# An RMSNorm-and-swish kernel: larger row groups, a first small store, and a different split of the squares

## The chip, the cores and the metric

The kernel runs on one core of one Trainium2 chip. The metric is the device time of one execution in microseconds (us). Of the kernel before, eight executions were timed: median 160.46 us, from 160.32 to 160.62.

## The reference

The input x has 16 x 1024 rows of 512 float32 values, 16,384 rows or 33.55 MB; the output has the same size. Each row is normalized by its root mean square, scaled by gamma and passed through swish:

```python
rms = np.sqrt(np.mean(x ** 2, axis=-1, keepdims=True) + eps)
x_norm = x / rms * gamma
return (x_norm * (1.0 / (1.0 + np.exp(-x_norm)))).astype(np.float32)
```

Every value is read once and written once, so 67.1 MB cross between HBM and SBUF.

## The kernel before, in words

**Tiles.** The 16,384 rows are 128 partitions times 128 rows. A tile of `sz` rows takes `128 * sz` neighbouring rows of x, of which each partition holds `sz` neighbours: one run of `sz` x 2 KB in HBM and in SBUF. There are eleven tiles, `sizes = [4, 4, 8] + [16] * 6 + [8, 8]` (line 30), each with one load and one store. All live in one ring buffer in SBUF, `xb`, with room for 96 rows per partition. The first eight tiles fill it; the last three (16, 8 and 8 rows) reuse room of earlier tiles, and their loads wait until the stores of those tiles have landed (`load`, lines 108 to 118).

**Chunks.** Computing goes by chunks of `cn = 4` rows per partition, 32 in all. For each chunk k:

- ScalarE squares one row with its accumulator, so that the sum of squares comes with it (line 159, scratch output `junk`), and squares the other `n_sq = 3` rows into PSUM (line 166, `sq`, two buffers).
- VectorE sums these three rows (`sums`, line 204).
- GpSimd adds eps (line 141) and raises to the power -1/2 (line 148).
- VectorE multiplies each of the four rows by its factor and by gamma (`norm`, line 215, four instructions).
- ScalarE applies swish in place (`swish`, line 178).

**Order.** It is written out by hand, one program per engine, with semaphores between them. ScalarE runs `square(k)`, then any store that is due, then `swish(k-2)` (lines 192 to 199). VectorE runs `sums(k)`, then `norm(k-1)` (lines 223 to 233). So the squares of a chunk run ahead of the swish of the chunk two before.

**Queues.** SyncE issues all loads, in the order of the tiles, on queue q1; the first two are placed ahead of the program's opening barrier. ScalarE issues all stores on queue q10, each when the last chunk of its tile has been through swish (`store`, line 181). Ahead of these, ScalarE's queue brings gamma (line 186): four copies of it to four partitions of `gamma4`, which GpSimd has set to zero first (line 136). VectorE spreads them over all partitions with a shuffle (line 228), which stands in its program right after `sums(0)` and before everything else; it waits for gamma's landing (`s_gld`).

At the end SyncE waits for the stores that no load has waited for (lines 236 to 238).

Of the kernel before, what the change touches and what calls it, by code (L numbers as in the profile page):

```python
# [8 lines left out]
@with_exitstack  # L9
def kernel(  # L10
    ctx: ExitStack,
    tc: tile.TileContext,
    x: bass.AP,
    gamma: bass.AP,
    eps: bass.AP,
    out: bass.AP,
):
    nc = tc.nc
    P = nc.NUM_PARTITIONS
    AF = mybir.ActivationFunctionType  # L20
    ALU = mybir.AluOpType
    fp32 = mybir.dt.float32
    bf16 = mybir.dt.bfloat16

    xf = x.flatten_outer_dims()
    of = out.flatten_outer_dims()
    R, D = xf.shape


    sizes = [4, 4, 8] + [16] * 6 + [8, 8]  # L30
    ring = 96
    early = 2
    cn = 4
    n_sq = 3
    N = sum(sizes)
    assert N * P == R, (N, R)


    tiles = []
    done = 0  # L40
    for sz in sizes:
        assert done % ring + sz <= ring
        tiles.append((done * P, sz, done % ring))
        done += sz
    T = len(tiles)

    chunks = [
        (t, r, r == at)
        for t, (_, sz, at) in enumerate(tiles)
        for r in range(at, at + sz, cn)  # L50
    ]
    K = len(chunks)
    ends = []
    e = 0
    for sz in sizes:
        e += sz // cn
        ends.append(e)

    inv_d = 1.0 / float(D)
    eps_f = float(eps)  # L60

    tc.close()
    tc.compile()  # L65

    def sbuf(name, shape, dt=fp32):
        return nc.alloc_sbuf_tensor(name, shape, dt).ap()

    xb = sbuf("xb", [P, ring, D])  # L70
    gamma4 = sbuf("gamma4", [P, D])
    gamma_sb = sbuf("gamma_sb", [P, D])
    junk = [sbuf(f"junk{i}", [P, D], bf16) for i in range(2)]
    neg_half = sbuf("neg_half", [P, cn])
    ms = sbuf("ms", [P, K, cn])
    aeps = sbuf("aeps", [P, K, cn])
    rstd = sbuf("rstd", [P, K, cn])
    sq = [nc.alloc_psum_tensor(f"sq{i}", [P, 4, D], fp32).ap() for i in range(2)]

    ld = [nc.alloc_semaphore(f"ld{t}") for t in range(T)]  # L80
    st = [nc.alloc_semaphore(f"st{t}") for t in range(T)]
    s_gld = nc.alloc_semaphore("s_gld")
    s_zero = nc.alloc_semaphore("s_zero")
    s_half = nc.alloc_semaphore("s_half")
    s_gamma = nc.alloc_semaphore("s_gamma")
    s_acc = nc.alloc_semaphore("s_acc")
    s_sq = nc.alloc_semaphore("s_sq")
    s_sum = nc.alloc_semaphore("s_sum")
    s_eps = nc.alloc_semaphore("s_eps")
    s_rstd = nc.alloc_semaphore("s_rstd")  # L90
    s_norm = nc.alloc_semaphore("s_norm")
    s_swish = nc.alloc_semaphore("s_swish")

    def need(ins, sem, value):
        return ins.wait_op(sem, value, "sem-ge")

    def dram(ap, t):
        first, sz, _ = tiles[t]
        return ap[first : first + P * sz].rearrange("(p n) d -> p n d", n=sz)

    def buf(t):
        _, sz, at = tiles[t]
        return xb[:, at : at + sz, :]


    stored_by_sync = set()

    def load(t):
        _, sz, at = tiles[t]
        waits = [  # L110
            u for u in range(t)
            if tiles[u][2] < at + sz and at < tiles[u][2] + tiles[u][1]
            and u not in stored_by_sync
        ]
        for u in waits:
            nc.sync.wait_ge(st[u], 16)
            stored_by_sync.add(u)
        return nc.sync.dma_start(out=buf(t), in_=dram(xf, t)).then_inc(ld[t], 16)  # L118

    entry = nc.main_func.blocks[0].instructions  # L120
    here = nc.cur_bb.bb.instructions
    for t in range(early):
        ins = load(t).ins
        assert here[-1] is ins or here[-1].name == ins.name
        here.pop()
        at = next(
            i for i, other in enumerate(entry)
            if other.engine == mybir.EngineType.SP
            and isinstance(other, mybir.InstDrain)
        )  # L130
        entry.insert(at, ins)
    for t in range(early, T):
        load(t)


    nc.gpsimd.memset(gamma4, 0.0).then_inc(s_zero, 1)  # L136
    nc.gpsimd.memset(neg_half, -0.5).then_inc(s_half, 1)  # L137
    nc.gpsimd.wait_ge(s_half, 1)
    for k in range(K):
        need(  # L140
            nc.gpsimd.tensor_scalar(  # L141
                out=aeps[:, k, :], in0=ms[:, k, :], scalar1=eps_f, scalar2=None,
                op0=ALU.add,
            ),
            s_sum, k + 1,
        ).then_inc(s_eps, 1)
        need(
            nc.gpsimd.tensor_tensor(  # L148
                out=rstd[:, k, :], in0=aeps[:, k, :], in1=neg_half, op=ALU.pow
            ),  # L150
            s_eps, k + 1,
        ).then_inc(s_rstd, 1)


    def square(k):
        t, at, first = chunks[k]
        if first:
            nc.scalar.wait_ge(ld[t], 16)  # L158
        acc = nc.scalar.activation(  # L159
            out=junk[k % 2], in_=xb[:, at + n_sq, :], func=AF.Square,  # L160
            scale=inv_d**0.5, accum_out=ms[:, k, n_sq : n_sq + 1],
        )
        if k >= 2:
            need(acc, s_acc, k - 1)
        acc.then_inc(s_acc, 1)
        square = nc.scalar.activation(  # L166
            out=sq[k % 2][:, 0:n_sq, :], in_=xb[:, at : at + n_sq, :],
            func=AF.Square, scale=inv_d**0.5,
        )
        if k >= 2:  # L170
            need(square, s_sum, k - 1)
        square.then_inc(s_sq, 1)

    def swish(k):
        _, at, _ = chunks[k]
        rows = xb[:, at : at + cn, :]
        need(
            nc.scalar.activation(out=rows, in_=rows, func=AF.Silu), s_norm, k + 1  # L178
        ).then_inc(s_swish, 1)

    def store(t):
        need(
            nc.scalar.dma_start(out=dram(of, t), in_=buf(t)), s_swish, ends[t]
        ).then_inc(st[t], 16)

    need(
        nc.scalar.dma_start(out=gamma4[0:P:32, :], in_=gamma.partition_broadcast(4)),
        s_zero, 1,
    ).then_inc(s_gld, 16)
    nc.scalar.preload_act_table_set("silu_and_others")  # L190
    stored = 0
    for k in range(K + 3):
        if k < K:
            square(k)
        while stored < T and ends[stored] <= k - 2:
            store(stored)
            stored += 1
        if 2 <= k < K + 2:
            swish(k - 2)


    def sums(k):
        need(
            nc.vector.tensor_reduce(  # L204
                out=ms[:, k, 0:n_sq], in_=sq[k % 2][:, 0:n_sq, :], op=ALU.add,
                axis=mybir.AxisListType.X,
            ),
            s_sq, k + 1,
        ).then_inc(s_sum, 1)

    def norm(k):
        _, at, _ = chunks[k]
        for j in range(cn):
            row = xb[:, at + j, :]
            ins = nc.vector.scalar_tensor_tensor(  # L215
                out=row, in0=row, scalar=rstd[:, k, j : j + 1], in1=gamma_sb,
                op0=ALU.mult, op1=ALU.mult,
            )
            if j == 0:
                need(ins, s_rstd, k + 1)  # L220
        ins.then_inc(s_norm, 1)

    for k in range(K + 1):
        if k < K:
            sums(k)
        if k == 0:
            need(
                nc.vector.stream_shuffle(gamma_sb, gamma4, [0] * 32), s_gld, 16  # L228
            ).then_inc(s_gamma, 1)
        if k == 1:  # L230
            nc.vector.wait_ge(s_gamma, 1)
        if k >= 1:
            norm(k - 1)


    for t in range(T):
        if t not in stored_by_sync:
            nc.sync.wait_ge(st[t], 16)

# [34 lines left out]
```

## Time and profile before

The profiled execution took 160.32 us; its span, from the first to the last instruction, is 159.0 us, so 1.32 us lie around it.

| What | Value |
|---|---|
| Median of 8 executions | 160.46 us |
| Profiled execution, its span | 160.32 us, 159.0 us |
| VectorE: norm, line 215, 128 times | 87.1 us, 737 ns each |
| VectorE: sum of three rows, line 204, 32 times | 55.8 us, 1744 ns each |
| ScalarE: swish of four rows, line 178, 32 times | 61.1 us, 1908 ns each |
| ScalarE: squares of three rows, line 166, 32 times | 45.9 us, 1433 ns each |
| ScalarE: square of one row and its accumulator's read, line 159, 32 times | 19.7 + 6.0 us, 615 + 186 ns each |
| DMA, mean over the span | 422 GB/s |
| ScalarE waiting for VectorE's norm | 17.6 us in 30 waits |
| VectorE waiting for ScalarE's squares | 9.8 us in 3 waits |
| SyncE waiting for stores ahead of the ring's reuse | 55.8 us (first), 18.9 us (second) |

How to read it: "busy" is the time in which an engine executes; DMA rows give the share in which the 16 DMA engines move packets, and the rate. A packet is one row run of one partition. The chain that ended last is followed back from the last instruction to whatever released each step. PE is not used.

### The profile page before, as it was taken

The page shows a single profiled execution, that of the slowest core. Times are in us where ns is not written, and L with a number is a line of the kernel's source. Part 1 is how long each engine was busy: PE and PEld are TensorE (multiplying, and loading weights), DVE is VectorE, ACT ScalarE, POOL GpSimd, SP SyncE. Part 2 cuts the span into 40 slices and gives each one's busy share as a digit, 9 for nine tenths or more (in the row PEclk, how much of TensorE's full clock was granted, in tenths as well). Part 3 has the DMA queues.
Part 4 walks back from the last instruction along what each step waited for, and adds up shares of the span by engine and source line. Part 5 has one row for each costly group of instructions (what it writes and reads, how often), then busy time and mean ns, then how long its engine had stood idle before and what let it go on. Part 6 is the DMA issues. An engine that isn't in the chain of part 4 may idle for free.

```text
span 159.0 us, 437 instructions
## 1 busy us (share of the span) xinstructions
DVE 139.2 (88%) x162; ACT 125.1 (79%) x129; POOL 78.6 (49%) x70
## 2 busy tenths in 40 slices
DVE  0298986999999999999999999999999999998600
ACT  1839839888888998888888888899888888883420
POOL 1043551445555554444444555555488888998100
DMA  6999989999989999999999999999999999999997
GB/s 260 435 495 396 396 371 480 402 422 453 437 367 482 449 416 431 437 437 404 445 429 439 437 445 412 412 457 433 433 416 429 433 441 453 420 429 437 400 412 309
DMA packets 3179, 67.14 MB, mean 422 GB/s; under 512 B 356, under 2 KB 356, under 8 KB 360
## 3 DMA queue, kind: packets, MB, share of 16 engines
q1 hardware_dynamic: 1584, 33.56, 49.8%
q10 hardware_dynamic: 1592, 33.56, 49.1%
q14 instruction: 3, 0.02, 0.0%
HBM read 33.56 MB, written 33.55 MB: 422 GB/s over the span
## 4 chain that ended last, share of the span: by engine, by line
DVE 76%; DMA 13%; ACT 2%; POOL 2%; issue 0%; SPq 0%; ACTq 0%
DVE xb L215 47%; DVE ms L204 29%; DMA xb<-in_x_dram 13%; POOL aeps L141 2%; ACT xb L178 1%; ACT sq L166 1%; POOL rstd L148 1%; ACT junk L159 0%; SPq L118 0%; ACTq L158 0%
## 5 line engine op out<-in xcount | busy, mean ns | idle before, releaser
L215 DVE SCALAR_TENSOR_TENSOR xb<-xb,rstd,gamma_sb 128x512 f32<-128x512 f32 x128 | 87.1, 737 | 1.2 <-POOL rstd L148 1.2
L178 ACT ACTIVATE xb<-xb 128x2048 f32<-128x2048 f32 x32 | 61.1, 1908 | 17.6 <-DVE xb L215 17.6
L141 POOL TENSOR_SCALAR aeps<-ms 128x4 f32<-128x4 f32 x32 | 36.6, 1144 | 64.6 <-DVE ms L204 64.6
L204 DVE TENSOR_REDUCE ms<-sq 128x3 f32<-128x1536 f32 x32 | 55.8, 1744 | 9.9 <-ACT sq L166 9.8
L166 ACT ACTIVATE sq<-xb 128x1536 f32<-128x1536 f32 x32 | 45.9, 1433 | 0.0
L148 POOL TENSOR_TENSOR rstd<-aeps,neg_half 128x4 f32<-128x4 f32 x32 | 41.2, 1288 | 2.7
L159 ACT ACTIVATE junk<-xb 128x512 bf16<-128x512 f32 x32 | 19.7, 615 | 5.9 <-DMA xb<-in_x_dram 5.9
L159 ACT ACTIVATION_READ_ACCUMULATOR junk<-xb 128x1 f32 x32 | 6.0, 186 | 0.0
L190 ACT ACT_TABLE_LOAD x1 | 1.3, 1283 | 3.6 <-issue 3.6
L136 POOL MEMSET gamma<- 128x512 f32 x1 | 0.5, 524 | 1.5 <-POOLq L65 1.5
L228 DVE STREAM_SHUFFLE gamma_sb<-gamma 128x512 f32<-128x512 f32 x1 | 0.7, 721 | 0.0
L255 POOL MEMSET const-float32-0.0<- 128x1 f32 x1 | 0.1, 98 | 0.2 <-issue 0.2
L255 POOL MEMSET const-uint8-127<- 128x1 uint8 x1 | 0.1, 103 | 0.0
L255 POOL MEMSET const-bfloat16-1.0<- 128x1 bf16 x1 | 0.1, 101 | 0.0
L137 POOL MEMSET neg_half<- 128x4 f32 x1 | 0.1, 101 | 0.0
L255 POOL MEMSET const-float32-1.0<- 128x1 f32 x1 | 0.1, 98 | 0.0
L228 DVE LOAD_MASK_SELECT gamma_sb<-gamma x1 | 0.0, 14 | 0.0
## 6 DMA issues: line engine op xcount, KB each, us to landing
xb<-in_x_dram SPq DMA_DIRECT2D x6, 4096.0 KB, 44.0
out_dram<-xb ACTq DMA_DIRECT2D x6, 4096.0 KB, 29.6
xb<-in_x_dram SPq DMA_DIRECT2D x3, 2048.0 KB, 37.7
out_dram<-xb ACTq DMA_DIRECT2D x3, 2048.0 KB, 10.1
xb<-in_x_dram SPq DMA_DIRECT2D x2, 1024.0 KB, 5.8
out_dram<-xb ACTq DMA_DIRECT2D x2, 1024.0 KB, 19.9
gamma<-in_gamma_dram ACTq DMA_DIRECT2D x1, 8.0 KB
```

The costliest lines, as they stand in the source:

```text
L136: nc.gpsimd.memset(gamma4, 0.0).then_inc(s_zero, 1)
L137: nc.gpsimd.memset(neg_half, -0.5).then_inc(s_half, 1)
L141: nc.gpsimd.tensor_scalar(out=aeps[:, k, :], in0=ms[:, k, :], scalar1=eps_f, scalar2=None, op0=ALU.add,),
L148: nc.gpsimd.tensor_tensor(out=rstd[:, k, :], in0=aeps[:, k, :], in1=neg_half, op=ALU.pow),
L159: acc = nc.scalar.activation(out=junk[k % 2], in_=xb[:, at + n_sq, :], func=AF.Square, scale=inv_d**0.5, accum_out=ms[:, k, n_sq : n_sq + 1],)
L166: square = nc.scalar.activation(out=sq[k % 2][:, 0:n_sq, :], in_=xb[:, at : at + n_sq, :], func=AF.Square, scale=inv_d**0.5,)
L178: nc.scalar.activation(out=rows, in_=rows, func=AF.Silu), s_norm, k + 1
L190: nc.scalar.preload_act_table_set("silu_and_others")
L204: nc.vector.tensor_reduce(out=ms[:, k, 0:n_sq], in_=sq[k % 2][:, 0:n_sq, :], op=ALU.add, axis=mybir.AxisListType.X,),
L215: ins = nc.vector.scalar_tensor_tensor(out=row, in0=row, scalar=rstd[:, k, j : j + 1], in1=gamma_sb, op0=ALU.mult, op1=ALU.mult,)
L228: nc.vector.stream_shuffle(gamma_sb, gamma4, [0] * 32), s_gld, 16
L255: nc = _bacc.Bacc("TRN2", target_bir_lowering=False, num_devices=1)
```

## The change

- **A scratch transfer.** An SBUF tile `blank` of 128 x 16 float32 is set to zero by GpSimd, as its first instruction. ScalarE's queue writes it to a scratch tensor in HBM ahead of gamma's transfer: 8 KB, 64 bytes per partition. SyncE waits for its landing after it has issued all loads.
- **Groups, loads and stores.** Rows are laid out in five groups of 16, 48, 32, 16 and 16 rows per partition. A load or a store moves a piece of a group: nine loads of 4, 4, 8, 16, 16, 16, 32, 16 and 16 rows; eight stores of 16, 32, 16, 16, 16, 16, 8 and 8 rows. The 32-row ones have runs of 64 KB per partition. A load waits for those stores that hold the room it will fill.
- **Squares.** In each third chunk (k % 3 == 2, ten of 32) ScalarE squares two rows with the accumulator, and two into PSUM for VectorE to sum; in the others one and three as before. The accumulator's semaphore is split in two, one per `junk` buffer.

```diff
-    sizes = [4, 4, 8] + [16] * 6 + [8, 8]
+    groups = [16, 48, 32, 16, 16]
     ring = 96
+    loads = [(0, 0, 4), (0, 4, 4), (0, 8, 8), (1, 0, 16), (1, 16, 16), (1, 32, 16),
+        (2, 0, 32), (3, 0, 16), (4, 0, 16)]
+    stores = [(0, 0, 16), (1, 0, 32), (1, 32, 16), (2, 0, 16), (2, 16, 16), (3, 0, 16),
+        (4, 0, 8), (4, 8, 8)]
     early = 2
     cn = 4
-    n_sq = 3
...
+    def n_sq(k):
+        return 2 if k % 3 == 2 else 3
...
+    scratch = nc.dram_tensor("scratch", [P, 16], fp32, kind="Internal").ap()
+    blank = sbuf("blank", [P, 16])
...
+    nc.sync.wait_ge(s_scratch, 16)
...
+    nc.gpsimd.memset(blank, 0.0).then_inc(s_blank, 1)
     nc.gpsimd.memset(gamma4, 0.0).then_inc(s_zero, 1)
...
     def square(k):
-        t, at, first = chunks[k]
-        if first:
-            nc.scalar.wait_ge(ld[t], 16)
-        acc = nc.scalar.activation(
-            out=junk[k % 2], in_=xb[:, at + n_sq, :], func=AF.Square,
-            scale=inv_d**0.5, accum_out=ms[:, k, n_sq : n_sq + 1],
-        )
-        if k >= 2:
-            need(acc, s_acc, k - 1)
-        acc.then_inc(s_acc, 1)
+        at, landing = chunks[k]
+        for i in landing:
+            nc.scalar.wait_ge(ld[i], 16)
+        n = n_sq(k)
+        for j in range(n, cn):
+            acc = nc.scalar.activation(
+                out=junk[j % 2], in_=xb[:, at + j, :], func=AF.Square,
+                scale=inv_d**0.5, accum_out=ms[:, k, j : j + 1],
+            )
+            last = acc_on[j % 2]
+            if last:
+                need(acc, s_acc[j % 2], last)
+            acc.then_inc(s_acc[j % 2], 1)
+            acc_on[j % 2] += 1
         square = nc.scalar.activation(
-            out=sq[k % 2][:, 0:n_sq, :], in_=xb[:, at : at + n_sq, :],
+            out=sq[k % 2][:, 0:n, :], in_=xb[:, at : at + n, :],
             func=AF.Square, scale=inv_d**0.5,
         )
...
+    need(nc.scalar.dma_start(out=scratch, in_=blank), s_blank, 1).then_inc(
+        s_scratch, 16
+    )
     need(
         nc.scalar.dma_start(out=gamma4[0:P:32, :], in_=gamma.partition_broadcast(4)),
         s_zero, 1,
```

## The prediction

> **What bounds the kernel now.** I read the engine shares first, then the DMA rows, then the chain that ended last, then windows and the timeline. From the page:
>
> ```profile
> DVE 139.2 (88%) x162; ACT 125.1 (79%) x129; POOL 78.6 (49%) x70
> ...
> DMA  6999989999989999999999999999999999999997
> ...
> q1 hardware_dynamic: 1584, 33.56, 49.8%
> q10 hardware_dynamic: 1592, 33.56, 49.1%
> ...
> DVE 76%; DMA 13%; ACT 2%; POOL 2%; issue 0%; SPq 0%; ACTq 0%
> ```
>
> The chain names VectorE, but the 16 DMA engines are busy 49.8 + 49.1 = 98.9% of the span: two limits stand nearly level. The windows (length, busy us of DVE, ACT and POOL, clock, DMA share, GB/s) say which of them sets the end:
>
> ```profile
> 17.00:21.00 4.00, 4.00 (x5) 3.04 (x2) 1.81 (x2) 1.00 1.01 362
> ...
> 30.00:100.00 70.00, 70.00 (x81) 62.75 (x65) 32.73 (x32) 1.00 1.01 434
> ...
> 152.00:154.00 2.00, 0.00 (x0) 0.24 (x1) 0.00 (x0) 1.00 0.94 401
> ```
>
> In 30 to 100 us both are full, at 434 GB/s. The last store leaves ScalarE's queue at 152.3 us, when the store before it still has packets until 153.8; DMA work never runs out but for a dent at 152 to 154. So the bytes set the end: 67.14 MB at 433 GB/s is 155.1 us. The trace's packet records have the first packet at 1.0 us and the last semaphore at 158.6, 0.4 before the span ends. The 3.5 us that are not bytes at full rate are: 1.0 before the first packet; about 0.8 of slow first packets up to 5 us; (433-362)/433 x 4 = 0.66 at 17 to 21; (433-401)/433 x 2 = 0.15 at 152 to 154; and 0.9 of smaller dents, packet overhead and the stagger of the engines' last packets (158.0 to 158.6).
>
> The dent at 17 to 21 follows the first store, issued at 16.21 to 16.57. The records show load packets of 32 KB, elsewhere 1213 ns, stretched up to 1985 ns on all 16 engines from 17.3 us, and the first store packet at 20.2. Gamma's small transfer, first on the same queue, left no such dent.
>
> [...] between 24 and 44 us, with loads of 32 KB rows and stores of 8 KB rows, the queues' shares are
>
> ```profile
> q1 hardware_dynamic: 231, 7.05, 82.0%
> q10 hardware_dynamic: 226, 1.65, 19.6%
> ```
>
> as many packets of each, so 4 to 1 in bytes.[...] gamma (issue over at 3.54, packet at 7.05) and the first store show about 3.6 under load, and I use 3.5.
>
> **The change part by part.**
>
> *Row sizes.* The packets took 309, 611 and 1213 ns for 8, 16 and 32 KB: 9 ns of overhead each and 36.7 ns per KB of 1000 B. Per engine, before has 32 packets of 8 KB and 48 of 16 KB; after, 16 and 24. Against 32 KB rows an 8 KB packet costs 23/4 ns too much and a 16 KB packet 4.5, so 0.09 + 0.11 us are saved. The 16 packets of 64 KB, extrapolated to 2417 ns, save 9 ns each, 0.14. No trace has a 64 KB row: at worst it runs at the rate of 32 KB rows (0), at best as said. I take -0.34.
>
> *Scratch transfer.* It adds 128 packets of 64 B, 8 per engine. The nearest row is the 4 B semaphore packet at 9 ns[...]. Estimate 8 x 11 = 0.09 us.[...] The wait on it by SyncE stands after all loads are issued (near 98 us), when it has long landed: 0.
>
> *The dent.* If the 0.66 us belong to the first write to HBM, the scratch transfer takes them with 64 B in flight instead of 8 KB rows, and they shrink to nothing or fall into the first 5 us. If they belong to a queue that starts anew beside loads, they stay, or come twice, since after the change the store queue runs empty once more. Bounds: -0.66 to +2.3 (rival C). I take -0.66, because the stretched packets end where the first write lands, and the last store, which finds that queue empty on some engines, shows no stretched packets (it has no loads beside it, which weakens this).
>
> *Two rows for three on VectorE.* Ten of 32 chunks (k = 2, 5, ... 29) reduce two rows instead of three. The reduction takes 1744 ns for 1536 elements, so about 533 less for 1024. ScalarE adds 0.61 (a square with accumulator and its read: 130.90 to 131.51 in the timeline) and saves 1908 - 1433 = 475 ns, the rows' price of 512 elements: +0.14. Now the loop from the end of a norm over swish and squares to the next reduction:
>
> ```profile
> 129.08 1.91 ACT L178 ACTIVATE xb<-xb 128x2048 f32<-128x2048 f32 x1 [0.46 <-DVE xb L215]
> 130.90 0.61 ACT L159 ACTIVATE junk<-xb 128x512 bf16<-128x512 f32 x1
> 131.42 0.19 ACT L159 ACTIVATION_READ_ACCUMULATOR junk<-xb 128x1 f32 x1
> 131.51 1.43 ACT L166 ACTIVATE sq<-xb 128x1536 f32<-128x1536 f32 x1
> 133.40 1.91 ACT L178 ACTIVATE xb<-xb 128x2048 f32<-128x2048 f32 x1 [0.45 <-DVE xb L215]
> ```
>
> ScalarE needs 3.98 of VectorE's 4.315 us (1.67 + 2.65 in the chain). With a short reduction VectorE needs 3.78 and ScalarE's 3.98 decides: 0.33 gained per such chunk, 9 of them between sums(4) and sums(31), 3.0 us. A chunk with two accumulated rows needs 4.12, still under 4.315. GpSimd's two steps end 1.30 after the norm before (the scale's addition overhangs by 0.15, then 0.09 and 1.04), later than a short reduction's 1.14, but 1.30 + 2.65 stays within the 3.98. The two accumulator semaphores add no work. This gain lies behind the full DMA; it only brings the last store forward, closing the dent at 152: -0.15.
>
> *Gamma, moved behind the scratch transfer.* ScalarE's queue issues the scratch transfer at about 2.05 (after a 0.1 us memset) to 3.1, if the first issue takes gamma's 1.09; then gamma's, and ScalarE starts some 0.4 later than 4.87. First scratch packet at 3.1 + 3.5 = 6.6. Its 8 packets and its semaphore each wait out one load packet: 8 turns of 0.61 + 0.01 to 11.6, then gamma and its semaphore at 1.21 each: 14.0, seen at 14.3, instead of 7.8. Queued behind the shuffle on VectorE is everything: shuffle 0.72, sums 1.68, norm 2.65, sums 1.14, norm 2.65, sums 1.67, norm 2.65, so sums(4) at 14.3 + 13.2 = 27.5 instead of 25.4. Then 27 periods, 116.5 - 3.0 = 113.5, and 10.3 from sums(31) to the last store (152.27 - 141.99): issue at 151.3 instead of 152.3. Cover: DMA has other stores queued. With 4.85 for 2.1 MB, 0.85 to the first packet and 0.4 to the end of the span, VectorE's chain alone would end the span at gamma + 143.1 = 157.4.
>
> *Loads and stores.* Store 0 (16 rows) waits for chunk 3, about 34 us, and shares evenly with the loads, then 1 to 2 with the 64 KB load; it lands by 58. The 32-row store waits for chunk 11: sums(12) at 27.5 + 8 x 4.2 = 61.1, norm and swish to 67. Bytes by 68 are (68 - 2) x 0.433 = 28.6 MB; less 4.2 of store 0 that is 24.4 of the 25.2 for the first 96 rows, and the 32-row load lands near 72 at half rate. Chunk 16 squares at 27.5 + 12 x 4.2 - 2.05 = 75.9: some 4 us of cover. The big store (8.4 MB, two thirds of 433 after 72) lands near 99; the last load, which SyncE holds until then, follows at half rate, 19.4 us, near 121; chunk 28 squares near 126. Both covers are thin, and a late load costs only beyond the 0.5 us between 157.4 and the bytes' end, as the queues never stand empty.
>
> Sum: 159.0 - 0.34 + 0.09 - 0.66 - 0.15 = 157.9 of span, 159.3 with the 1.32 around it (profiled 160.32). The median, 160.46, is 0.14 above: 159.4.
>
> **Rivals.**
> B, the dent stays, at store 0 or around the scratch transfer: 0.66 back, 160.1. For it: one dent in either kernel. Against it: the scratch transfer has 64 B per packet.
> C, slower: every start of the store queue beside loads dents, at store 0 (33 us) and at the 32-row store (66 us). Each costs 0.66, up to half of the 3 us before the first write, 1.5, as the queues now share evenly. A's 159.4 has none of them, so this is 159.4 + 1.3 to 3.0, 160.7 to 162.4, likely 161. It turns slower once the dents sum to over 1.4. Gamma's silence speaks against it, but gamma writes no HBM.
> D, slower: gamma lands late and VectorE's chain sets the end, at gamma + 143.1 of span. It decides over the bytes from 14.8 us on, and the kernel is slower from 16.2; at 18, 161.1 + 1.5 = 162.6. For it: nothing lies between VectorE and that wait. Against it: the scratch packets would have to wait two turns each.
> That 5.3 us of reduction saved shorten the kernel by as much, to 157, needs bytes at over 433 GB/s; no chance.
>
> **How the numbers follow.** A 0.46 (159.4; 159.1 to 159.8), B 0.20 (160.1; 159.8 to 160.4), C 0.18, D 0.16. The bound of what the measurement tells is 0.2%, 0.32 us: faster is under 160.14, slower over 160.78. A, a half of B and 0.01 of D are faster, 0.57; the other half of B and 0.06 of C the same, 0.16; the rest slower, 0.27. The range from 159.0 to 161.3 leaves out C's and D's upper parts.
>
> **What would show it.** Right: no dent near 33 us; the GB/s rows at 433 until the last store; VectorE's idle time larger (waiting for gamma by some 5 us, for ScalarE by 0.2 in each third chunk); the reduction of two rows near 1.2 us; ScalarE never waiting for the 32-row load. Wrong: dents after 33 and 66 us (C); the shuffle later than 15 us, or a gap in DMA before the last store (D); a wait for loads of over 2 us at chunk 16 or 28.

## The result and the profile after

The changed kernel takes 162.80 us (median of 11 executions, 161.20 to 163.55) against 160.40 for the kernel before: a ratio of 1.0137, with a 95% interval from 1.0116 to 1.0159. It is slower, where 159.4 us and a gain of 0.7% were forecast, and it lies outside the range of 159.0 to 161.3. Its executions also spread over 2.3 us, those of before over 0.65. Every ratio here is formed from all executions but those more than 1.5% above the fastest of the same kernel, so it need not be the quotient of the two medians beside it; the one of the changed kernel takes in a twelfth execution, of 161.87 us.

The profiled execution took 162.08 us, its span 160.8. From the page of the changed kernel: engine shares, DMA, queues, the chain that ended last.

```profile
DVE 134.5 (84%) x162; ACT 126.4 (79%) x149; POOL 65.4 (41%) x71
...
DMA  7999999999999989989999998999999999999992
...
q1 hardware_dynamic: 1296, 33.56, 49.4%
q10 hardware_dynamic: 1304, 33.57, 48.5%
...
DVE 55%; ACT 25%; DMA 5%; issue 4%; another core or an unknown queue 3%; POOL 0%; ACTq 0%; POOLq 0%
```

VectorE lost 4.7 us of work, and the DMA engines were busy for 97.9% of a longer span. Summed over the 16 engines the packets took 157.29 us per engine, exactly as before (157.29): the mean DMA engine had no more to do. The chain names VectorE and ScalarE, as it follows the last instruction back and does not ask which DMA engine landed last. The last digit of the DMA row, 7 before and 2 after, is the first hint. The windows of the tail show it (length, busy us of DVE, ACT, POOL, clock, DMA share, GB/s), first of the kernel before:

```profile
157.00:158.60 1.60, 0.00 (x0) 0.00 (x0) 0.00 (x0) 1.00 0.48 205
158.60:162.00 3.40, 0.00 (x0) 0.00 (x0) 0.00 (x0) 1.00 0.00 0
```

and then of the changed kernel:

```profile
157.00:158.60 1.60, 0.00 (x0) 0.00 (x0) 0.00 (x0) 1.00 0.29 123
158.60:160.80 2.20, 0.00 (x0) 0.00 (x0) 0.00 (x0) 1.00 0.03 15
```

In the changed kernel most engines are done earlier, and something goes on after 158.6 us at a twentieth of the rate or less. The packet records of the trace say what: the last store's semaphores come from 15 engines between 157.4 and 158.5 us, and from one at 160.39. One engine of 16, a late engine, ends 2.6 us after the median one.

Two more windows of the changed kernel, for the dent after the first real store:

```profile
17.00:21.00 4.00, 3.85 (x5) 4.00 (x5) 2.02 (x2) 1.00 0.91 393
33.00:37.00 4.00, 4.00 (x6) 3.31 (x5) 2.04 (x2) 1.00 1.07 369
```

Windows of 4 us count whole packets, so that their GB/s wander; the packet records are sharper. A packet is called stretched where it takes longer than its usual 309, 611, 1213 or 2418 ns for 8, 16, 32 or 64 KB. The records show no stretched packet at 14 to 24 us in the changed kernel (0.66 us per engine before) and 0.91 us per engine at 30 to 40. The dent has moved to the new first store, issued at 30.4, and has grown.

Last, ScalarE at chunk 16, which needs the 32-row load, and VectorE behind it (timeline; in brackets the idle time ahead and what ended it):

```profile
76.63 0.63 ACT L178 ACTIVATE junk<-xb 128x512 bf16<-128x512 f32 x1 [4.55 <-DMA xb<-in_x_dram]
...
78.72 1.76 DVE L229 TENSOR_REDUCE ms<-sq 128x3 f32<-128x1536 f32 x1 [4.04 <-ACT sq L187]
```

The load lands at 76.2 us. Its last packet had ended at 73.8; the semaphore packet behind it waited out one store packet of 64 KB, 2.4 us. Even so the last store leaves at 150.98, earlier than before (152.27): this stall is not yet what sets the end.

### The profile page after: what moved, and what is told of

It is laid out like the page before. It is cut to its first block, busy times and chain, and to the rows that moved or that the text cites. A ratio compares the mean times of both kernels' runs of the same rounds, so it can differ in the third digit from the quotient of the medians.

```text
span 160.8 us, 451 instructions
## 1 busy us (share of the span) xinstructions
DVE 134.5 (84%) x162; ACT 126.4 (79%) x149; POOL 65.4 (41%) x71
## 4 chain that ended last, share of the span: by engine, by line
DVE 55%; ACT 25%; DMA 5%; issue 4%; another core or an unknown queue 3%; POOL 0%; ACTq 0%; POOLq 0%
DVE xb L240 35%; DVE ms L229 20%; ACT xb L199 12%; ACT sq L187 9%; DMA gamma<-in_gamma_dram 5%; ACT junk L178 4%; DVE gamma_sb L253 0%; POOL gamma L151 0%; POOL blank L150 0%; ACTq L175 0%; POOLq L69 0%
## 5 line engine op out<-in xcount | busy, mean ns | idle before, releaser
L199 ACT ACTIVATE xb<-xb 128x2048 f32<-128x2048 f32 x32 | 60.9, 1904 | 12.9 <-DVE xb L240 12.9
L229 DVE TENSOR_REDUCE ms<-sq 128x3 f32<-128x1536 f32 (+1 forms) x32 | 50.7, 1586 | 12.5 <-ACT sq L187 11.0
L156 POOL TENSOR_SCALAR aeps<-ms 128x4 f32<-128x4 f32 x32 | 20.6, 644 | 76.1 <-DVE ms L229 76.1
L163 POOL TENSOR_TENSOR rstd<-aeps,neg_half 128x4 f32<-128x4 f32 x32 | 44.0, 1376 | 2.7
L187 ACT ACTIVATE sq<-xb 128x1536 f32<-128x1536 f32 (+1 forms) x32 | 41.6, 1299 | 0.0
L178 ACT ACTIVATE junk<-xb 128x512 bf16<-128x512 f32 x42 | 25.8, 615 | 8.0 <-DMA xb<-in_x_dram 8.0
L178 ACT ACTIVATION_READ_ACCUMULATOR junk<-xb 128x1 f32 x42 | 7.8, 187 | 0.0
```

What stands on the lines that cost most here:

```text
L156: nc.gpsimd.tensor_scalar(out=aeps[:, k, :], in0=ms[:, k, :], scalar1=eps_f, scalar2=None, op0=ALU.add,),
L163: nc.gpsimd.tensor_tensor(out=rstd[:, k, :], in0=aeps[:, k, :], in1=neg_half, op=ALU.pow),
L178: acc = nc.scalar.activation(out=junk[j % 2], in_=xb[:, at + j, :], func=AF.Square, scale=inv_d**0.5, accum_out=ms[:, k, j : j + 1],)
L187: square = nc.scalar.activation(out=sq[k % 2][:, 0:n, :], in_=xb[:, at : at + n, :], func=AF.Square, scale=inv_d**0.5,)
L229: nc.vector.tensor_reduce(out=ms[:, k, 0 : n_sq(k)], in_=sq[k % 2][:, 0 : n_sq(k), :], op=ALU.add, axis=mybir.AxisListType.X,),
```

## The experiments

All ratios are against the kernel before, with 95% intervals; the changed kernel stands at 1.0137. Times are medians unless a single execution is named.

### Which part of the change

**Without the scratch transfer.** The four lines that write it, wait for it and clear its source are taken out.

```diff
-    need(nc.scalar.dma_start(out=scratch, in_=blank), s_blank, 1).then_inc(
-        s_scratch, 16
-    )
```

> The changed kernel without the scratch transfer. The changed kernel stands at 1.014 of before; in its profile 15 DMA engines end at 157.4 to 158.1 us and one at 160.4. Theory S (the scratch transfer brings the late engine): 1.003 or less. Theories R (the 64 KB rows bring it) and F (the first real store, now 16 rows of 32 KB, brings it): 1.012 to 1.016, the late engine still 2 us or more behind the rest.

Measured: 163.01 us, 1.0152 (1.0107 to 1.0197). Two engines end late, the last 3.4 us after the median. Theory S falls.

**The squares as before.**

```diff
-        return 2 if k % 3 == 2 else 3
+        return 3
```

> The changed kernel with three rows summed by VectorE in every chunk, as before. S, R and F: the split of the squares is not the cause, 1.012 to 1.018, the upper end because the last store then leaves some 2 us later. If the denser ScalarE program is the cause: 1.004 or less.

Measured: 161.73 us, 1.009 of the 160.23 us of the kernel before beside it; the 20 executions lie anywhere from 160.3 to 164.0, and the 12 below 162.7 alone give 1.0052 (1.0031 to 1.0072). Neither expectation fits: the split of the squares is not needed for the loss, since half of it or more remains in 11 of the 20, but six stay below 161 us, where the changed kernel has none of 12. This version comes back below.

**The 32-row pieces split.**

```diff
-        (2, 0, 32), (3, 0, 16), (4, 0, 16)]
-    stores = [(0, 0, 16), (1, 0, 32), (1, 32, 16), (2, 0, 16), (2, 16, 16), (3, 0, 16),
+        (2, 0, 16), (2, 16, 16), (3, 0, 16), (4, 0, 16)]
+    stores = [(0, 0, 16), (1, 0, 16), (1, 16, 16), (1, 32, 16), (2, 0, 16), (2, 16, 16), (3, 0, 16),
```

> The changed kernel with the 32-row load and the 32-row store each split in two of 16 rows; the layout of the groups stays. R: 0.998 to 1.004, the late engine gone. S and F: 1.012 to 1.016.

Measured: 160.60 us, 1.0018 (1.0009 to 1.0027), 160.2 to 161.2. Most of the loss is gone with the 64 KB rows, and so is the tail:

```profile
157.00:158.60 1.60, 0.00 (x0) 0.00 (x0) 0.00 (x0) 1.00 0.58 246
158.60:162.00 3.40, 0.00 (x0) 0.00 (x0) 0.00 (x0) 1.00 0.00 0
```

**The scratch transfer alone, added to the kernel before.**

> The kernel before with the scratch transfer alone added. S: 1.008 or more, with one late engine. R and F: 0.998 to 1.003, gamma's shuffle about 2 us later as in the changed kernel (10.8 us), and the dent at 17 to 21 us still there at about 0.66 us, since the dent after the first store stayed in the changed kernel.

Measured: 160.24 us, 0.9996 (0.9985 to 1.0008): nothing. One of its 12 executions, not in the ratio, took 162.51 us, as long as the changed kernel and without any 64 KB rows; it was not profiled, so its cause is open. The dent did change, against the expectation: at 14 to 24 us it fell from 0.66 to 0.28 us per engine. But the stretched packets of the first 10 us rose from 0.41 to 0.68, and those at 43 to 49 from 0.09 to 0.36. All in all the packets of this profile are stretched by 1.66 us per engine, those of before by 1.41. In these profiles, one of each kernel, the transfer moves the loss about and takes none away.

**The split of the squares alone, added to the kernel before.**

> The kernel before with the changed split of the squares alone (two rows summed by VectorE in each third chunk). If DMA sets the end, as the prediction has it: 0.996 to 1.001, the last store issued 1 to 3 us earlier and the time not following. If VectorE sets it: 0.980 to 0.988.

Measured: 160.39 us, 0.9990 (0.9979 to 1.0002). The last store leaves at

```profile
148.35 0.34 ACTq L192 DMA_DIRECT2D out_dram<-xb  x1
```

3.9 us before the 152.27 of the kernel before, and the time does not follow. So DMA sets the end of the kernel before, as the prediction read it.

### Load or store

**Only the load split, the 64 KB store kept.**

> The changed kernel with the 32-row load split in two of 16, the 32-row store kept. Theory RS (the late engine comes from the store of 64 KB rows): 1.010 to 1.016, with store packets of 64 KB stretched by 0.2 to 0.7 us on one or two engines, which end 2 us or more after the rest. Theory RL (it comes from the load of 64 KB rows): 0.999 to 1.004, all engines within 1 us.

Measured: 162.67 us, 1.0135 (1.0112 to 1.0158), as much as the whole change. Four engines end over 1 us late, the last 3.1 us after the median. Fourteen of the 128 store packets of 64 KB, elsewhere 2418 ns, were stretched by 0.11 to 1.15 us. The tail:

```profile
157.00:158.60 1.60, 0.00 (x0) 0.00 (x0) 0.00 (x0) 1.00 0.48 205
158.60:162.00 3.40, 0.00 (x0) 0.00 (x0) 0.00 (x0) 1.00 0.11 48
```

As the load is split here, its wait at chunk 16 (4.55 us) has no part in the loss of the whole change: it is hidden.

**Only the store split, the 64 KB load kept.**

> The changed kernel with the 32-row store split in two of 16, the 32-row load kept. RS: 0.999 to 1.004, no late engine. RL: 1.010 to 1.016. Either way ScalarE waits for the 32-row load at chunk 16; if that wait is what costs the time, 1.010 or more with no late engine.

Measured: 161.65 us, 1.0069 (1.0048 to 1.0090), and all 16 engines end between 160.0 and 160.14. This loss has another cause, the third named in the expectation, though it costs less than said there:

```profile
79.84 0.63 ACT L178 ACTIVATE junk<-xb 128x512 bf16<-128x512 f32 x1 [7.58 <-DMA xb<-in_x_dram]
...
81.94 1.76 DVE L229 TENSOR_REDUCE ms<-sq 128x3 f32<-128x1536 f32 x1 [7.07 <-ACT sq L187]
```

The 16-row store starts sooner than the 32-row one (issued at 47.0 and, for its second half, 64.2 us) and shares the engines with the 64 KB load for longer; ScalarE waits until all of this load has landed, and the wait at chunk 16 grows from 4.55 to 7.58 us. (In the changed kernel the packets of loads and stores take turns: on its late engine the eleven data packets that begin at 77 to 98 us alternate between the two queues.) The last store leaves at 154.21 instead of 150.98, and now VectorE's chain sets the end. The split store costs ScalarE 3 us more of waiting, and with no late engine to hide it, the wait shows.

**Long rows alone, in the kernel before.**

```diff
-    sizes = [4, 4, 8] + [16] * 6 + [8, 8]
+    sizes = [4, 4, 8, 16, 32, 32, 16, 8, 8]
```

> The kernel before with four of its 16-row tiles joined to two of 32 rows, so that two loads and two stores have 64 KB rows; no scratch transfer, squares as before. RS: 1.010 to 1.025, as two such stores give a late engine twice the chance. If the late engine needs the changed kernel's other parts: 0.998 to 1.004.

Measured: 164.20 us, 1.0234 (1.0211 to 1.0258). The size is as RS has it, the reason is not: all engines end within 0.4 us of the median one, which ends at 162.2, and the last store leaves only at 155.16, after loads that landed late (ScalarE waited up to 4.8 us at once). But 49 of its 256 store packets of 64 KB were stretched by over 0.1 us, all beside loads of 16 KB rows and on about half of the engines. The run shows that long rows alone are enough for a loss, and doesn't tell the two ways apart.

### What stretches the packets

In the trace's packet records, each store packet is put with the shortest load row that ran at its side (within some 1.3 us):

| Store rows | Load rows beside them | Runs | Stretched over 0.1 us | Mean stretch |
|---|---|---|---|---|
| 64 KB | none | last 32 rows alone (below) | 0 of 128 | 10 ns |
| 64 KB | 64 KB | equal rows (below) | 0 of 77 | 0 ns |
| 64 KB | 32 KB | only the load split | 14 of 128 | 41 ns |
| 64 KB | 16 KB | short loads (below) | 26 of 96 | 120 ns |
| 32 KB | 16 KB | before | 1 of 292 | 1 ns |
| 32 KB | 16 KB | the split of the squares alone | 7 of 292 | 7 ns |
| 32 KB | 16 KB | short loads (below) | 40 of 384 | 32 ns |
| 32 KB | 8 KB | four to one (below) | 1 of 454 | 2 ns |

**A 64 KB store with nothing beside it:** the last 32 rows as one store, all other pieces of 16 rows or fewer.

> The changed kernel with all rows of 32 KB but for the last 32 rows, which leave as one store of 64 KB rows when all loads have landed. The last store of 8.4 MB then begins at 151 us and takes 19.4: about 171 to 172 us, which is not the point. Theory M (long store rows are stretched only beside loads with shorter rows): no packet of 64 KB over 2.55 us, all engines end within 1 us. Theory A (they are stretched by themselves): some over 2.6 us and an engine 1 us or more late.

Measured: 173.5 us in one execution (that the end comes later is the size of the last store). None of its 64 KB packets was stretched by more than 44 ns, and all engines end within 0.2 us. Theory A falls.

**Shorter loads beside the 64 KB store:** loads of 16 rows, the last two of them in four of 8.

> The changed kernel with the 32-row load in two of 16 rows and the last two 16-row loads in four of 8 rows, so that the store of 64 KB rows meets loads of 16 KB rows. M: more packets stretched than beside 32 KB rows (a mean of 0.1 us and more over the 128), ratio 1.013 to 1.030. A: as beside 32 KB rows, a mean of 0.04 us, 1.010 to 1.016.

Measured: 166.52 us; 1.0336 (1.0278 to 1.0393) without the slowest of the four executions, 167.15; more than expected. The stretch is more than twice that beside 32 KB rows, 0.09 us in the mean over the 128, just under M's 0.1 (120 ns over the 96 beside 16 KB rows), and far from A's 0.04. The 32 KB stores that followed were stretched too, 40 of 384 packets, where the kernel before has 1 of 292. But in the split of the squares alone, which has no 64 KB rows at all, 7 of 292 were stretched as well, by up to 0.44 us: such rows aren't the only ones to be stretched, and whether they bring on the stretch of those that follow is not shown. The time, though, is that of late loads (at 85 to 115 us the load queue moved 3.74 MB in 260 packets, the store queue 8.62 MB in as many):

```profile
DVE ms L230 <- ACT sq L188: 18.8, 5, 7.2
ACT junk L179 <- DMA xb<-in_x_dram: 15.0, 5, 7.5
```

(waits: total, times, longest). The last store leaves at 158.77.

**Four to one with shorter rows:** stores of 32 KB rows, the last two loads in eight of 4 rows.

> The changed kernel with 16-row pieces in place of the 32-row ones and its last two 16-row loads in eight of 4 rows: stores of 32 KB rows beside loads of 8 KB rows, four to one as 64 KB beside 16 KB. Theory Q (the ratio of the rows stretches): stretched store packets, a mean of 0.05 us and more, a late engine, 1.008 or more. Theory N (only rows of 64 KB are stretched): a mean under 0.02 us, all engines within 1 us and no later than 0.5% beyond the version with 16-row pieces, unless the loads, with a fifth of the rate, come too late for ScalarE; then VectorE's waits show it.

Measured: 162.76 us, 1.0150 (1.0129 to 1.0170). The store packets are not stretched (2 ns) and all engines end within 0.1 us: N holds in this run (the two runs with stretched 32 KB packets beside 16 KB rows show that its "only" goes too far). What costs the time is the exception that was named, loads too late for ScalarE, which waits for them for 12.9 us, 7 times.

**Equal rows:** groups of 32, 32, 32, 16 and 16 rows. The 32-row store is the first; beside it runs the 64 KB load, then nothing, as the next load waits for this store.

> The changed kernel with the same number of 64 KB rows, but its groups are 32, 32, 32, 16, 16 rows and the 32-row store is the first one: it begins beside the 64 KB load and, once that has landed, is alone, as the next load waits for it. Theory M (64 KB store rows are stretched only beside shorter load rows): no 64 KB store packet over 2.6 us after the first dent, all engines within 1 us at the end, 0.998 to 1.005. Theory L (any 64 KB store row makes an engine late): 1.010 or more, with an engine 2 us behind.

Measured: 161.24 us, 1.0053 (1.0036 to 1.0070). None of the 128 store packets of 64 KB was stretched by over 0.1 us, as M has it, though this store is also the first one here, so that more differs than the rows beside it. The time lies just over the upper end, and one engine is 1.4 us late, which M had not. Its packets say that no store did this: at 48 us it fetched instructions (0.31 us), the load packet behind took 0.64 us longer, and a load packet in the dent after the first store 1.92 us. This dent is larger here: around 50 us, load packets of 64 KB took up to 1.9 us longer, 1.43 us per engine in the mean.

### Is it the late engine that makes the time

The version with three rows has three further profiled executions.

> The changed kernel with three rows summed in every chunk, looked at again: its executions lay between 160.3 and 164.0 us, and the one profiled, at 160.4, had no late engine. If the late engine makes the time: where this execution takes 161.5 us or more, one or more engines end 1.5 us or more after the median one, and the span exceeds the median engine's end by the same; at 161 or less, all end within 1 us.

> As the run before: in the profiled execution the time over some 158.4 us equals the delay of the last DMA engine behind the median one plus 1.7 us, if the late engine makes the time.

> As the two runs before: a late engine of 1.5 us or more where the execution takes 161.5 us or more, none where it takes 161 or less.

The first two came out as expected: at 162.90 and 162.86 us, the last engine ends 3.6 and 3.0 us after the median one. The third, at 161.11, falls between the two limits; its last engine is 1.6 us late. The profiled executions, with the landing of the last store on the median and on the last DMA engine, times in us:

| Version | Time | Median engine | Last engine | Time less last engine | 64 KB store packets stretched over 0.1 us |
|---|---|---|---|---|---|
| before | 160.32 | 158.1 | 158.6 | 1.7 | none there |
| changed | 162.08 | 157.8 | 160.4 | 1.7 | 2 |
| three rows (e2) | 160.40 | 157.9 | 158.6 | 1.8 | 0 |
| three rows (e16) | 161.11 | 157.8 | 159.4 | 1.7 | 0 |
| three rows (e15) | 162.86 | 158.2 | 161.2 | 1.7 | 11 |
| three rows (e14) | 162.90 | 157.7 | 161.2 | 1.7 | 7 |
| no scratch | 162.98 | 157.9 | 161.3 | 1.7 | 8 |
| 16-row pieces | 160.19 | 158.1 | 158.5 | 1.7 | none there |

One and the same kernel takes 160.4 or 162.9 us; its median engine ends within 0.5 us of the same moment, and the time is the landing of the last engine plus 1.7. (The 158.4 of the second expectation was too high by 0.3 to 0.8.) The tail of the profiled execution in e2, at 160.40, and then of the one in e14, at 162.90:

```profile
157.00:158.60 1.60, 0.00 (x0) 0.00 (x0) 0.00 (x0) 1.00 0.36 154
158.60:162.00 3.40, 0.00 (x0) 0.00 (x0) 0.00 (x0) 1.00 0.00 0
```

```profile
157.00:158.60 1.60, 0.00 (x0) 0.00 (x0) 0.00 (x0) 1.00 0.36 154
158.60:161.60 3.00, 0.00 (x0) 0.00 (x0) 0.00 (x0) 1.00 0.06 27
```

The first lines are equal to the last digit; all of the 2.5 us lies in what one or two engines do in the second. In e14 stretched store packets follow one another on the last engine, 0.69 us at 84.9, 0.63 at 89.2, 0.27 at 93.5, and on the engine that ends last but one a 32 KB load packet took 0.76 longer at 98.4. In e16, without stretched store packets, two load packets of 32 KB, at the moment when the 64 KB store ends (99 us), took 0.88 and 0.99 us longer.

The records don't name the engine of a packet, but a packet begins within a few ns of the end of the one before it on its engine (3 or 4 ns before that end in all 165 packets of the changed kernel's late engine, from 1.1 us on), so the packets of an engine can be strung together. In the changed kernel every engine then has the same 16 data packets of 64 KB, 80 of 32, 24 of 16 and 16 of 8: none takes work off an engine that has fallen back, and all are busy to the end. The changed kernel's late engine, followed back from 160.39 to 32 us, lost 1.16 us in two stretched store packets of 64 KB (87 and 91 us), 0.84 in a fetch of instructions at 46.2 us and the load packet behind it, and 0.83 in three more load packets (71, 99 and 117 us). The stretched stores are thus less than half of its 2.6 us. The same 0.84 in the version with 16-row pieces left no late engine.

There is a lead to what starts it. Seven of the profiles have 64 KB stores beside 32 KB loads. In five (changed, no scratch, only the load split, e14, e15) a fetch at 46.2 or 46.3 us is followed by a load packet that takes 0.53 us longer, and 2 to 14 store packets of 64 KB are stretched later. In the other two (e2, e16) that fetch comes at 47.5 or 47.6 us, ahead of a store packet, and none is stretched. No run moved the fetch, so this is not shown to be the cause.

### All of the change but the rows

**The kernel before with the scratch transfer and the split of the squares.**

> The kernel before with the scratch transfer and the split of the squares, the tiles as they were: all of the change but the groups, loads and stores. If the row sizes carry the whole loss: 0.996 to 1.000; if the other two lose something together: 1.002 or more.

Measured: 160.11 us, 0.9990 (0.9978 to 1.0002). The groups, loads and stores carry the whole loss. This is the lowest median of all, but not told apart from the kernel before: no version run here clearly beats it.

## Why the prediction was wrong

**The step that failed: row sizes.** "At worst it runs at the rate of 32 KB rows (0), at best as said. I take -0.34." The sizes themselves were right: a 64 KB packet takes 2418 ns (2417 forecast), and without stretch the packets of the changed kernel take 155.61 us per engine against 155.89, 0.28 less. What was missing is a bound on the other side, and on single engines: with the 64 KB store as the only long piece the term is +2.3 us (162.67 against 160.40, 1.0135), and without any 64 KB rows 1.0018 is left. The store packets of 64 KB, and the loads at their end, were stretched by up to a microsecond on some engines only. Spread over 16 engines that is 0.08 us in the changed kernel's store packets, nothing; on the engine that takes it, it is 1.2 us, and with what else that engine lost, it is the end of the kernel.

**The sum was made for a mean engine.** It put the bytes' end at 157.9 of span less 0.4, that is 157.5; the median engine landed at 157.8. The stagger of the engines' ends, 0.6 us before, was put among the losses as if it were fixed. That the bytes can move no faster was the author's estimate from the 434 GB/s of 30 to 100 us; the changed kernel moved 426 there, its dent included.

**The dent.** -0.66 was taken; in the two profiles it is +0.25 (0.66 to 0.91 per engine), which is on the side of rivals B and C. The reason given, that the dent belongs to the first write to HBM, fell: a first write of 64 B lands at 9.3 us, and the dent comes after it all the same, with or without the scratch transfer (0.91 and 0.91). Its size seems to go with the rows that meet, though it varies from profile to profile: 0.66 and 0.75 for a first store of 8 KB beside loads of 32 KB (before, the split alone), 0.75 to 1.15 for 32 beside 32 (12 profiles), 1.43 for 64 beside 64 (one). C's second dent, at the 32-row store, did not come: no packet at 65 to 70 us is stretched by over 0.08 us. That later start of the store queue beside loads costs nothing.

**VectorE and ScalarE: right.** The groups by form, of the changed kernel:

```profile
L229 DVE TENSOR_REDUCE ms<-sq 128x2 f32<-128x1024 f32 x10 | 12.2, 1215 | 0.0
L187 ACT ACTIVATE sq<-xb 128x1024 f32<-128x1024 f32 x10 | 10.1, 1006 | 0.0
```

1215 ns (1211 forecast) and 1006 (958). The last store was put at 151.3 and left at 150.98; that this work lies behind the DMA was confirmed by the split alone (0.9990).

**Gamma: turns right, start wrong.** Rival D did not decide. The shuffle ran at

```profile
10.76 0.01 DVE L253 LOAD_MASK_SELECT gamma_sb<-gamma  x1 [2.00 <-DMA gamma<-in_gamma_dram]
```

not at 14.3. The packets of 64 B took 11 ns, as estimated (the 9 ns of a packet's overhead and 64 B at 36.7 ns per KB give as much), and one turn each, as forecast. But the scratch issue took 0.35 us instead of gamma's 1.09, so that its first packet came at 5.5 instead of 6.6, and half its turns were those of 8 KB load packets (0.31 us).

**The 32-row load.** It was put at 72 us with some 4 us of cover. VectorE ran 3.5 us earlier than forecast, so the store it shares with and the need for it came earlier too; its data were there at 73.8, it landed at 76.2, as its semaphore had to wait out a store packet of 64 KB, which the forecast had not counted, and it was waited for, 4.55 us. That it adds nothing to the whole change is shown by the run with the load split; that a longer wait for it (7.58 us) costs when no engine is late, by the run with the store split.

The mechanism that the forecast had on the other side (C or D) was not what happened. "Slower" had 0.27, and none of it was for an engine falling behind the others.

## What to carry to other kernels

In this kernel, where DMA is busy to the end, the end is that of the slowest DMA engine, not of the mean. For a kernel like it: look at how the engines' last packets stagger, and at the spread of the executions, before costing an edit by bytes and rate. Joining two rows to one saved 7 to 9 ns here (309, 611, 1213 and 2418 ns for 8, 16, 32 and 64 KB); past 32 KB, in this kernel, longer rows cost more than they save where stores of such rows share the engines with shorter load rows (1.0135 with one such store). ScalarE waited for a load of one long piece until all of it had landed (4.55 us, and 7.58 with the store split), and a semaphore packet behind it waited out a store packet of 64 KB, 2.4 us: both ends of that trade have to be put on the timeline.

## What the runs showed of the hardware that was not expected

- A store packet of 64 KB takes 2418 ns alone or beside 64 KB loads, and was stretched by up to 1.15 us beside 32 KB loads (1.41 beside 16 KB), on some engines and in some executions only; packets of 32 KB beside 8 KB were not (1 of 454), so the ratio of the rows alone is not the reason, and some of 32 KB beside 16 KB were (40 of 384 and 7 of 292), so 64 KB is no clean limit. What does this, which engine it falls on, and whether the denser ScalarE program makes it more frequent (none of 12 executions below 161 us, against six of 20 with three rows), stays open.
- A packet costs less per byte the longer its row, up to 32 KB (309 ns for 8 KB, 1213 for 32) and for a 64 KB packet by itself (2418 ns); for the kernel, though, the step to 64 KB costs time: 1.0135 with one such store.
- Three fetches of instructions of 8 KB run on single DMA engines in each profile (309 ns, and the load or store packet after it mostly 0.2 to 0.5 us longer, up to 0.64).
- The first store of a kernel cost load packets 0.7 to 1.4 us per engine before its own first packet in most profiles, the most with the longest rows. After an earlier small write it was smaller with 8 KB rows (0.28) and not with 32 KB rows (0.91 with and without), and the sum over the profile was no less (1.66 us per engine against 1.41).
